# A gated embedding's product in seven block products instead of eight, on one Trainium2 core

## The chip, the cores and the metric

The kernel runs on one core of a Trainium2 chip. The metric is the time of one execution in device microseconds (us); lower is better. The engines are TensorE (PE, its weight loads PEld), VectorE (DVE), ScalarE (ACT), GpSimd (POOL) and the queue SP, which issues every DMA here.

## The reference, cut to what matters

One layer of an encoder for 1024 tokens of width 1024: two attention groups of eight heads each, then the output projection and a gated embedding for each token. All is float32. The last three lines are the part that the change concerns:

```
y = concat([sb_y, mla_y], axis=-1) @ w_out[i]
x = x + rms_norm(y, norm_post_g[i])

ple = rms_norm(p[i] @ w_ple[i], ple_norm_g[i])
x = x + ple * sigmoid(x @ w_ple_gate[i] + b_ple_gate[i])
```

The product `x @ w_ple_gate` is 1024x1024 by 1024x1024.

## The kernel before, in words

**Numbers in two parts.** TensorE multiplies in the type fp32r. To keep float32 accuracy each operand is split (`split`): a high part (a cast to fp32r) and a low part (the operand less its high part). A product then takes three matmuls: high by high, high by low, low by high. A matmul has a stationary operand of 128x128 (the tokens) and a moving one of up to 512 columns (the weight), and sums into a PSUM bank.

**A plan written before the program.** The kernel's code does not issue instructions: a `Recorder` notes each with the tiles that it reads and writes, and `schedule` then lists them for each engine by a model of their costs. An instruction's priority is its place in the recorded order, moved by a few constants (`LOW`, `AHEAD`, `URGENT`). SBUF is handed out by the same plan: 28 slots of 4 KB per partition named `u`, 10 named `f`, and 4 large ones named `h16` (rows show `h`). A slot can hold two halves of 2 KB. PSUM has 3 banks `a` and 5 banks `t`. Each engine, SP too, executes its list in order.

**The stages.** First come the input norm and projections, then the attention, in 32 units (`SEQ` lists 16 pairs), with projections, loads and the first of the output products woven between them (`FILL0`, `RATES`). At the end of the attention stands the tail, whose order is the list `TAIL`:

- a step `oT` (`e1`) is the output projection of token tile T (128 tokens): for each half of 512 columns 24 matmuls (8 blocks of the inner dimension, 3 each), then the norm and the residual; the weight lies split in the four `h16` slots. For tiles 4 to 7 the operand `ys1` lies in eight `u` slots until the last of them is done.
- a step `eT` is the gated embedding of tile T. `e2a` transposes the tile (8 transposes of 128x128 into two `t` banks) and splits it. `e2b` makes for each half 24 matmuls and then, in turn, DVE adds the bias, ACT takes the sigmoid, POOL multiplies by `pl` and adds to `x2`, and SP stores. In the last tile DVE does what POOL does elsewhere, and the last half is closed in two pieces of 256 columns.
- `wg_gen` loads the gate's weight in eight rows of blocks (512 KB each) and splits each: a cast of 128x1024 and a subtraction of 128x1024.

`choice(i)` gives an elementwise instruction to DVE where `SPLITS[i]` is 1 and to POOL where it is 0. All instructions are recorded through one line, L517, so groups in the profile are told apart by engine, operation and tile (`a` and `t` are PSUM; `u`, `f`, `h` SBUF).

Of the kernel before, what the change touches and what calls it, by code (L numbers as in the profile page):

```python
# [12 lines left out]
F32 = mybir.dt.float32  # L13
# [3 lines left out]
AF = mybir.ActivationFunctionType  # L17
ALU = mybir.AluOpType
# [5 lines left out]
D = 1024  # L24
NT = 8
# [85 lines left out]
class Access:  # L111
# [408 lines left out]
def block_kernel(ctx, tc, x, p, positions, norm_pre_g, w_in, q_norm_g, w_uq, kv_norm_g, w_ukv,  # L520
# [4 lines left out]
    PE, ACT, DVE, POOL, SP = R.PE, R.ACT, R.DVE, R.POOL, R.SP  # L525
# [12 lines left out]
    ps_a, ps_t, ps_s, ps_v, ps_l = (bank(k) for k in "atsvl")  # L538
# [30 lines left out]
    ident = const([128, 128], "ident")  # L569
# [17 lines left out]
    ple_d = dram([S, D], "ple_d")  # L587
# [11 lines left out]
    mm = PE.matmul  # L599
    half = [slice(0, 512), slice(512, 1024)]  # L600
# [17 lines left out]
    def choice(i):  # L618
        return DVE if SPLITS[i] else POOL

    def bcast(dst, src, n):
        SP.dma_start(dst, src[0:1, :].broadcast_to([128, n]))
        return dst

    def load_split(shape, src, name, leng=None, heng=None):

        raw = k4(shape, F32, name + "r")
        SP.dma_start(raw, src)
        wh, wl = k4(shape, name=name + "h"), k4(shape, name=name + "l")
        split(wh, wl, raw, leng=leng or POOL, heng=heng)  # L630
        return wh, wl
# [85 lines left out]
    gb = {}  # L717
# [512 lines left out]
    wo, wg = [[], []], [[], []]  # L1230

    def wo_gen():
        gb["post"] = bcast(k4(dt=F32, name="gb_post"), norm_post_g, D)
        for g in range(2):
            wo[0].append(h16(name="woh"))
            wo[1].append(h16(name="wol"))
            for k in range(4):
                raw = k4(dt=F32, name="wo_r")
                SP.dma_start(raw, w2o[:, 4 * g + k])
                split(wo[0][g][:, k], wo[1][g][:, k], raw, leng=choice(7 + k % 2))  # L1240
                yield 0.0

    def wg_gen():
        for k in range(8):
            h_, l_ = load_split((128, 1024), w2g[:, k], "wg", leng=choice(9 + k % 3))
            wg[0].append(h_)
            wg[1].append(l_)
            yield 0.0
        gb["b"] = bcast(k4(dt=F32, name="gb_b"), b_ple_gate, D)

    def big(lhs, w_h, w_l):

        def mms(ps, n):
            for kb in range(KB):
                lh, ll = lhs(kb)
                mm(ps, lh, w_h(kb, n), start=(kb == 0), stop=False)
                mm(ps, lh, w_l(kb, n), start=False, stop=False)
                mm(ps, ll, w_h(kb, n), start=False, stop=(kb == KB - 1))
                if kb in (2, 5):
                    yield 1.95  # L1260
            yield 1.3
        return mms

    x2s, x2t, yin = {}, {}, {}

    def y_load(t):
        ts = slice(t * 128, (t + 1) * 128)
        if t < 4:
            yt = [k4((128, 4, 2, 128), name="yin") for _ in range(2)]
            for g in range(2):  # L1270
                SP.dma_start(f(yt[g]), y_d[t, :, 4 * g:4 * g + 4])
            ys = lambda kb: [yt[kb // 4][:, kb % 4, a] for a in range(2)]
        else:
            ys = lambda kb: [ys1[kb][:, t - 4, a] for a in range(2)]
        xt = k4(dt=F32, name="x2")
        SP.dma_start(xt, x[0, ts, :])
        yin[t] = (ys, xt)

    def e1(t, keep):
        ys, xt = yin.pop(t)  # L1280
        mms = big(ys, lambda kb, n: wo[0][kb // 4][:, kb % 4, half[n]], lambda kb, n: wo[1][kb // 4][:, kb % 4, half[n]])
# [11 lines left out]
    def x2_load(t):  # L1293
        xt = k4(dt=F32, name="x2r")
        SP.dma_start(xt, x2_d[t * 128:(t + 1) * 128, :])
        x2s[t] = xt

    def e2a(t):
        x2 = x2s[t]
        xs = [[k2((128, 4, 128), name="x2t") for _ in range(2)] for _ in range(2)]  # L1300
        for g in range(2):
            ps = ps_t()
            for k in range(4):
                kb = g * 4 + k
                PE.transpose(ps[:, k * 128:(k + 1) * 128], x2[:, kb * 128:(kb + 1) * 128], ident)
            split(xs[0][g], xs[1][g], ps.rearrange("q (k n) -> q k n", k=4), heng=ACT)
        x2t[t] = xs

    def e2b(t):
        ts = slice(t * 128, (t + 1) * 128)  # L1310
        pl = k4(dt=F32, name="pl")
        SP.dma_start(pl, ple_d[ts, :])
        xs = x2t.pop(t)
        mms = big(lambda kb: [xs[a][kb // 4][:, kb % 4] for a in range(2)], lambda kb, n: wg[0][kb][:, half[n]], lambda kb, n: wg[1][kb][:, half[n]])
        x2 = x2s.pop(t)
        last = t == NT - 1
        eng = DVE if last else POOL
        for n in range(2):
            ps = ps_a()
            for _ in mms(ps, n):  # L1320
                pass
            w = 256 if last and n else 512
            for c0 in range(0, 512, w):
                v = slice(512 * n + c0, 512 * n + c0 + w)
                sg = k2((128, w), F32, "sgz")
                DVE.tensor_tensor(sg, ps[:, c0:c0 + w], gb["b"][:, v], ALU.add)
                ACT.activation(sg, sg, AF.Sigmoid)
                eng.tensor_tensor(pl[:, v], pl[:, v], sg, ALU.mult)
                eng.tensor_tensor(x2[:, v], x2[:, v], pl[:, v], ALU.add)
                SP.dma_start(out[0, ts, v], x2[:, v])  # L1330

# [3 lines left out]
    weave = Weaver(R)  # L1335
# [11 lines left out]

    for item in FILL0:
        fill(item)
# [19 lines left out]
    for u, (i, s) in enumerate(units):  # L1369
# [13 lines left out]
    for _ in range(5):  # L1383
        run_later(True)
    weave.drain()
    weave.add("wg", wg_gen(), False)
    R.front = True
    for t in range(N1, 4):
        for _ in e1_gen(t):
# [1 line left out]
    y_load(4)  # L1391
    R.front = False
    weave.drain()
    for step in TAIL:
        k, t = step[0], int(step[1])
        if k == "x":
            x2_load(t)
        elif k == "e":
            if t < 4 and t not in x2s:
                x2_load(t)  # L1400
            e2a(t)
            e2b(t)
        else:
            R.front = True
            if t + 1 < NT:
                y_load(t + 1)
            for _ in e1(t, True):
                pass
            R.front = False
    R.issue(tc)  # L1410

# [26 lines left out]
```

## Time and profile before

| what | value |
|---|---|
| median of 3 runs | 787.84 us (787.14 to 790.75) |
| the profiled execution, its own time | 793.85 us |
| its span, first to last instruction | 792.1 us |
| PE busy | 768.9 us (97%), 3948 matmuls |
| DVE, ACT, POOL busy | 537.6, 394.6, 330.1 us |
| granted TensorE clock, mean | 0.997 of full speed |

How to read it: the span is that of one execution under the profiler; the medians are of runs without it. A busy share is a mean over stages. Matmuls overlap one another, so the time that one costs in a row of many is read from start to start, not from its duration. A row of a group ends with the idle time before its instructions and what ended it.

### The profile page before, as it was taken

To read this page: it belongs to the slowest core of one execution; us is meant where nothing else is said; L and a number is where in the kernel's file an instruction comes from. 1 tells how busy PE (TensorE), PEld (TensorE's weight loads), DVE (VectorE), ACT (ScalarE), POOL (GpSimd) and SP (SyncE) were. 2 spreads that over 40 slices of the span, in tenths; PEclk is the share of its full clock that TensorE was granted. 3 is DMA by queue.
4 is the path that set the end of the run, shared out by engine and by line. 5 is a ranking of instruction groups with operands and counts; after the bars stand their busy time and mean duration, and the time that the engine had idled before them with its cause. 6 is when DMAs were issued, how large, how long until landed. Compare 5 with 4: busy or idle time off the path is not lost.

```text
span 792.1 us, 11714 instructions
## 1 busy us (share of the span) xinstructions
PE 768.9 (97%) x3948; PEld 634.2 (80%) x3948; DVE 537.6 (68%) x1006; ACT 394.6 (50%) x961; POOL 330.1 (42%) x318
## 2 busy tenths in 40 slices
PE   5999989999999999999998999999999999999997
PEld 3887879988888877888887787888888888888885
DVE  5775215489837869887987999999689886222222
ACT  5415124234526586676557777775966731211211
POOL 5654224102422259779877521010485140034342
PEclk9999999999999999999999999999999999999999
DMA  9544451158998636365545787685366365212311
GB/s 340 196 145 130 144 174 46 54 209 330 345 336 267 202 130 215 121 225 160 180 153 187 242 270 241 209 300 190 118 204 209 123 224 173 60 73 72 129 67 53
DMA packets 97166, 143.45 MB, mean 181 GB/s; under 512 B 7249, under 2 KB 54865, under 8 KB 97106
## 3 DMA queue, kind: packets, MB, share of 16 engines
q1 hardware_dynamic: 97106, 142.70, 53.9%
q8 instruction: 31, 0.51, 0.3%
q14 instruction: 29, 0.24, 0.1%
HBM read 96.02 MB, written 46.66 MB: 180 GB/s over the span
## 4 chain that ended last, share of the span: by engine, by line
PE 86%; DMA 6%; DVE 5%; ACT 2%; issue 1%; SPq 1%; DVEq 0%; ACTq 0%
PE a L517 61%; PE t L517 24%; DVE u L517 2%; DVE f L517 1%; ACT u L517 1%; DMA u<-q_d 1%; DMA f<-in_w_in_dram 1%; DMA y_d<-u 1%; DVE nm L517 1%; DMA q_d<-f 1%; SPq L517 1%; DMA u<-in_norm_pre_g_dram 1%; DMA k_d<-f 1%; ACT f L517 0%; DMA q_d<-u 0%
## 5 line engine op out<-in xcount | busy, mean ns | idle before, releaser
L517 POOL TENSOR_TENSOR u<-u,u 128x512 f32<-128x512 f32 (+17 forms) x155 | 216.1, 1405 | 165.6 <-ACT u L517 81.9
L517 PE MATMUL a<-h,f 128*128 128x512 f32 x864 | 239.6, 405 | 0.2 <-DVE f L517 0.2
L517 PE MATMUL a<-u,u 128*128 128x512 f32 (+2 forms) x762 | 188.4, 378 | 1.3 <-DVE u L517 0.6
L517 PEld LDWEIGHTS a<-h,f 128*128 128x128 f32 x864 | 155.7, 189 | 27.9 <-DVE f L517 0.5
L517 DVE TENSOR_TENSOR u<-t,u 128x512 fp32r<-128x512 f32 (+4 forms) x280 | 146.4, 554 | 25.2 <-ACT u L517 23.4
L517 PEld LDWEIGHTS a<-u,u 128*128 128x128 f32 x762 | 137.7, 188 | 29.1 <-DVE u L517 2.3
L517 ACT CAST u<-t 128x512 fp32r<-128x512 f32 (+3 forms) x256 | 113.4, 492 | 94.9 <-PE t L517 79.0
L517 PE MATMUL t<-u,u 128*128 128x512 f32 (+4 forms) x576 | 152.4, 370 | 4.5 <-DMA u<-q_d 4.2
L517 PE MATMUL t<-ident,u 128*128 128x128 f32 x792 | 126.5, 275 | 2.4 <-ACT u L517 1.7
L517 PEld LDWEIGHTS t<-u,u 128*128 128x128 f32 x576 | 102.7, 190 | 23.6 <-DMA u<-q_d 5.2
L517 PEld LDWEIGHTS t<-ident,u 128*128 128x128 f32 x792 | 97.3, 141 | 23.7 <-DVE u L517 5.1
L517 ACT ACTIVATE u<-t 128x384 f32<-128x384 f32 (+5 forms) x208 | 91.1, 518 | 46.3 <-PE t L517 35.0
L517 DVE TENSOR_TENSOR u<-a,u 64x512 f32<-64x512 f32 (+4 forms) x59 | 37.5, 642 | 80.5 <-PE a L517 67.3
L517 DVE TENSOR_TENSOR_SCAN u<-u 128x64 f32<-128x64 f32 (+3 forms) x64 | 69.4, 1094 | 27.4 <-ACT u L517 24.4
L517 ACT ACTIVATE f<-a 128x512 bf16<-128x512 f32 (+2 forms) x64 | 34.6, 542 | 81.1 <-PE a L517 70.5
L517 DVE TENSOR_TENSOR f<-a,f 128x512 f32<-128x512 f32 (+2 forms) x54 | 34.4, 644 | 51.4 <-ACT f L517 48.9
L517 PE MATMUL a<-h,u 128*128 128x512 f32 x288 | 68.9, 395 | 0.0
L517 ACT ACTIVATE u<-t,nms 128x384 f32<-128x384 f32 (+4 forms) x96 | 55.1, 581 | 21.7 <-DVE nms L517 19.5
L517 PEld LDWEIGHTS a<-h,u 128*128 128x128 f32 x288 | 53.9, 188 | 12.7 <-ACT u L517 0.3
L517 POOL MEMSET u<- 128x128 f32 x64 | 12.5, 208 | 106.0 <-PE t L517 38.2
L517 DVE TENSOR_REDUCE nm<-t 128x1 f32<-128x384 f32 (+4 forms) x96 | 51.8, 547 | 1.5 <-PE t L517 0.7
L517 PE MATMUL a<-u,h 128*128 128x512 f32 x192 | 51.7, 417 | 1.0 <-DVE h L517 1.0
(95 smaller groups left out, 710.5 us busy)
## 6 DMA issues: line engine op xcount, KB each, us to landing
u<-q_d SPq DMA_DIRECT2D x64, 256.0 KB, 4.6
u<-k_d SPq DMA_DIRECT2D x16, 512.0 KB, 6.3
u<-v_d SPq DMA_DIRECT2D x16, 512.0 KB, 5.3
f<-in_w_in_dram SPq DMA_DIRECT2D x14, 512.0 KB, 5.0
v_d<-u SPq DMA_DIRECT2D x12, 512.0 KB, 3.4
f<-in_x_dram SPq DMA_DIRECT2D x9, 512.0 KB, 6.5
k_d<-u SPq DMA_DIRECT2D x9, 512.0 KB, 3.7
q_d<-u SPq DMA_DIRECT2D x9, 512.0 KB, 4.8
```

The lines of the kernel that those rows point to most:

```text
L517: x["fn"](*[place(a) for a in x["args"]], **{k: place(a) for k, a in x["kw"].items()})
```

## The change

Two token tiles are now taken together. With the pair's operand in blocks A11, A12 (first tile, first and second half of the inner dimension), A21, A22 (second tile), and the weight's four 512x512 blocks B11, B12, B21, B22, the four output blocks are made of seven products of blocks instead of eight:

```
S1 = A21+A22   S2 = S1-A11   S3 = A11-A21   S4 = A12-S2
T1 = B12-B11   T2 = B22-T1   T3 = B22-B12   T4 = B21-T2
P1 = A11 B11   P2 = A12 B21   P3 = S4 B22   P4 = A22 T4   P5 = S1 T1   P6 = S2 T2   P7 = S3 T3
out11 = P1+P2            out12 = P1+P6+P5+P3
out21 = P1+P6+P7+P4      out22 = P1+P6+P7+P5
```

(P4's sign is in T4, which is recorded as B21-T2.) Each product is 12 matmuls of 512 columns (4 blocks, 3 matmuls each). Every sum is split in high and low again. The code, cut:

```
-TAIL = ("x1", "o4", "o5", "o6", "x2", "x3", "o7", "e3", "x0", "e4", "e0", "e1", "e5", "e2", "e6", "e7")
+TAIL = ("o4", "w1", "w2", "o5", "a4", "o6", "w3", "x1", "x0", "x2", "e4", "a0", "e0", "a6", "x3", "e6", "a2", "e2")
-SEQ = (... (2, 1), (5, 0), (5, 1), (7, 1), (4, 1), (1, 1), (6, 1))
+SEQ = (... (2, 1), (5, 0), (7, 1), (5, 1), (4, 1), (1, 1), (6, 1))
...
 wo_gen:
+        for n in range(2):
+            for a in wo:
+                a.append(h16((128, 8, 512), name="wo"))
             for k in range(4):
+                SP.dma_start(raw, w2o[:, 2 * k:2 * k + 2, half[n]])
...
+    def wg_part(i):
+        if i == 1:
+            for k in range(4):
+                SP.dma_start(raw, w2g[:, k::4, half[0]])
+                SP.dma_start(b12, w2g[:, k, half[1]])
+                split(h_, l_, raw, leng=choice(9), heng=ACT if SPLITS[10] else DVE)
+                choice(25).tensor_tensor(b12, b12, raw[:, 0], ALU.subtract)
+                split(t1[:, 0], t1[:, 1], b12, leng=choice(26), heng=ACT if SPLITS[10] else DVE)
+            return
+        h_, l_ = (h16((128, 4, 2, 512), name="wgs") for _ in range(2))
+        for a, nm in enumerate((("T4", "T2") if i == 2 else ("T3", "B22"))):
+            wg[nm] = [(h_[:, k, a], l_[:, k, a]) for k in range(4)]
+        for k in range(4):
+            SP.dma_start(ra, w2g[:, k::4, half[1]])
+            if i == 2:
+                SP.dma_start(rb, w2g[:, k::4, half[0]])
+                choice(27).tensor_tensor(ra[:, 0], ra[:, 0], rb[:, 0], ALU.subtract)
+                choice(28).tensor_tensor(ra[:, 1], ra[:, 1], ra[:, 0], ALU.subtract)
+                choice(29).tensor_tensor(ra[:, 0], rb[:, 1], ra[:, 1], ALU.subtract)
+            else:
+                choice(30).tensor_tensor(ra[:, 0], ra[:, 1], ra[:, 0], ALU.subtract)
+            split(h_[:, k], l_[:, k], ra, leng=choice(31 if i == 2 else 32), heng=ACT if SPLITS[11] else DVE)
...
 e2a (16 transposes of a pair into four t banks, then):
+        parts("A11", ps[0, 0], ACT, DVE)
+        ACT.copy(f11, ps[0, 0])
+        ACT.copy(f21, ps[1, 0])
+        DVE.tensor_tensor(s1, ps[1, 1], f21, ALU.add)
+        parts("S1", s1, ACT, choice(33))
+        parts("A12", ps[0, 1], ACT, DVE)
+        choice(34).tensor_tensor(s2, s1, f11, ALU.subtract)
+        parts("S2", s2, ACT, choice(35))
+        DVE.tensor_tensor(s4, ps[0, 1], s2, ALU.subtract)
+        parts("S4", s4, ACT, choice(36))
+        choice(37).tensor_tensor(f11, f11, f21, ALU.subtract)
+        parts("S3", f11, ACT, choice(38))
+        parts("A22", ps[1, 1], ACT, DVE)
...
 e2b (products in the order 1, 2, 6, 5, 3, 7, 4; close = bias or sum, sigmoid, times pl, plus x2, store):
+            if i == 4 and last:
+                for v in (slice(0, 256), slice(256, 512)):
+                    close(1, 0, product(xs, 4, v), w, w, v, DVE)
+            if i == 1:
+                ACT.copy(p1, ps)
+                DVE.tensor_tensor(p1b, ps, b0, ALU.add)
+            elif i == 2:
+                close(0, 0, ps, p1b, p1b)
+            elif i == 6:
+                DVE.tensor_tensor(u2, ps, p1, ALU.add)
+                choice(41).tensor_tensor(w, u2, b0, ALU.add)
+                choice(42).tensor_tensor(u2, u2, b1, ALU.add)
+            elif i == 5:
+                DVE.tensor_tensor(u2, ps, u2, ALU.add)
+            elif i == 3:
+                close(0, 1, ps, u2, p1)
+            elif i == 7:
+                DVE.tensor_tensor(w, ps, w, ALU.add)
+                close(1, 1, ps, u2, u2)
+            else:
+                close(1, 0, ps, w, w)
```

In the tail a step `wN` is `wg_part(N)`, `aT` is `e2a` and `eT` is `e2b` of the pair T, T+1; the pairs come in the order 4, 0, 6, 2, and `o6` and `o7` are recorded half by half in turn. DVE does choices 9, 25 to 27, 31, 35, 38, 41 and 42; POOL 28 to 30, 32 to 34, 36, 37, 39 and 40; the casts of the weight go to ACT. Besides `SEQ`, two neighbours change places in `FILL0` twice, `RATES` differs in four late entries, and three entries of `SPLITS` move instructions of the stages before the tail. `URGENT` changes as well.

TensorE, the last output half and the first products. Before, in the middle of the first tile of the gated embedding (the rows of one half, both operands in `u`):

```order
L517 MATMUL a_343<-u_6187,u_6580 128x512
L517 MATMUL a_343<-u_6213,u_6580 128x512
L517 MATMUL a_343<-u_6187,u_6580 128x512
L517 MATMUL a_343<-u_6258,u_6580 128x512
L517 MATMUL a_343<-u_6284,u_6580 128x512
```

Now, in the first pair, products 6 (its end), 5, and the beginnings of 3, 7 and 4; `u_6517` is S1, `u_6576` S4, `u_6586` S3, `u_6594` A22; `h_1` and `h_3` hold the high and low parts of T3 and B22, `h_0` and `h_2` those of T4 and T2:

```order
L517 MATMUL a_343<-h_0_202,u_6571 128x512
L517 MATMUL a_214<-u_6220,u_6517 128x512 x3
...
L517 MATMUL a_214<-u_6386,u_6517 128x512 x3
L517 MATMUL a_290<-h_1_391,u_6576 128x512
L517 MATMUL a_290<-h_3_402,u_6576 128x512
L517 MATMUL a_290<-h_1_391,u_6576 128x512 x2
L517 MATMUL a_290<-h_3_402,u_6576 128x512
L517 MATMUL a_290<-h_1_391,u_6576 128x512 x2
L517 MATMUL a_343<-h_1_391,u_6586 128x512
L517 MATMUL a_343<-h_3_402,u_6586 128x512
```

A half's 24 matmuls in one bank have become products of 12 in a bank each, and in this pair the products 3, 7 and 4 stand among one another, so that their third and fourth blocks come late.

POOL, from the end of the output projections on. Before (`hsr` is the norm of an output tile, the rows behind them the closing of the first tile):

```order
L517 TENSOR_TENSOR hsr_4225<-hsm_4169,nhalf 128x1
L517 TENSOR_TENSOR hsr_4006<-hsm_3985,nhalf 128x1
L517 TENSOR_TENSOR u_6534<-u_6534,u_6611 128x512
L517 TENSOR_TENSOR u_6402<-u_6402,u_6534 128x512
L517 TENSOR_TENSOR u_6534<-u_6534,u_6611 128x512
```

Now (`u_6597`, `u_6602`, `u_6611`, `u_6606` are the four blocks of the weight part w3; the rows to `h_3` make the low parts of T3 and B22; `u_6640` and `f_5971` close the pair's first tile):

```order
L517 TENSOR_TENSOR hsr_4225<-hsm_4169,nhalf 128x1
L517 TENSOR_TENSOR u_6597<-u_6597 128x512
L517 TENSOR_TENSOR hsr_4006<-hsm_3985,nhalf 128x1
L517 TENSOR_TENSOR u_6602<-u_6602 128x512
L517 TENSOR_TENSOR h_3_402<-u_6597,h_1_391 128x1024
L517 TENSOR_TENSOR h_3_402<-u_6602,h_1_391 128x1024
L517 TENSOR_TENSOR u_6611<-u_6611 128x512
L517 TENSOR_TENSOR u_6606<-u_6606 128x512
L517 TENSOR_TENSOR h_3_402<-u_6611,h_1_391 128x1024
L517 TENSOR_TENSOR h_3_402<-u_6606,h_1_391 128x1024
L517 TENSOR_TENSOR u_6640<-u_6640,u_6682 128x512
```

Four sums and four low parts of the weight now stand on POOL ahead of every closing.

TensorE at the program's end. Before, the last tile's last half:

```order
L517 MATMUL a_343<-u_6382,u_7019 128x512
L517 MATMUL a_343<-u_6393,u_7019 128x512
L517 MATMUL a_343<-u_6382,u_7026 128x512
L1434 UNCONDITIONAL_BRANCH
```

Now, the end of product 7 of the last pair and product 4 in two halves of 256 columns:

```order
L517 MATMUL a_343<-h_1_391,u_6963 128x512
L517 MATMUL a_214<-h_0_202,u_7118 128x256
L517 MATMUL a_214<-h_2_220,u_7118 128x256
L517 MATMUL a_214<-h_0_202,u_7118 128x256 x2
...
L517 MATMUL a_290<-h_2_220,u_7118 128x256
L517 MATMUL a_290<-h_0_202,u_7118 128x256
L1547 UNCONDITIONAL_BRANCH
```

The last 12 matmuls of 512 columns have become 24 of 256. In all, TensorE's list loses 60 matmuls of 512 columns and gains 24 of 256; the number of transposes stays.

## Rows read from the trace of the kernel before

**Rows 1.** The page: busy time, granted clock in 40 slices, chain that ended last.
```profile
PE 768.9 (97%) x3948; PEld 634.2 (80%) x3948; DVE 537.6 (68%) x1006; ACT 394.6 (50%) x961; POOL 330.1 (42%) x318
PEclk9999999999999999999999999999999999999999
PE 86%; DMA 6%; DVE 5%; ACT 2%; issue 1%; SPq 1%; DVEq 0%; ACTq 0%
```

**Rows 2.** Busy time of each engine in stretches of the tail, clock, DMA share, GB/s.
```profile
633.00:692.00 59.00, 58.98 (x276) 48.02 (x275) 35.85 (x53) 12.04 (x31) 10.62 (x8) 1.00 0.46 152
715.00:740.00 25.00, 25.00 (x126) 20.77 (x123) 6.12 (x10) 5.13 (x10) 10.33 (x8) 1.00 0.28 87
```

**Rows 3.** TensorE's longest waits in the whole span (in all, times, longest).
```profile
PE t L517 <- DMA u<-in_norm_pre_g_dram: 7.2, 1, 7.2
PE t L517 <- DMA u<-q_d: 4.2, 3, 1.9
```

**Rows 4.** TensorE in order of time, one tile of the gated embedding (start, us).
```profile
714.73 1.58 PE L517 MATMUL t<-ident,u 128*128 128x128 f32 x13
716.07 11.33 PE L517 MATMUL a<-u,u 128*128 128x512 f32 x48
727.24 0.49 PE L517 MATMUL t<-ident,u 128*128 128x128 f32 x3
727.49 11.32 PE L517 MATMUL a<-u,u 128*128 128x512 f32 x48
```

**Rows 5.** TensorE in order of time, matmuls of 256 columns in the attention.
```profile
461.56 0.64 PE L517 MATMUL a<-u,u 128*128 128x256 f32 x4
462.04 0.71 PE L517 MATMUL t<-ident,u 128*128 128x128 f32 x5
```

**Rows 6.** POOL and DVE in order of time, beside each other and POOL nearly alone.
```profile
648.77 1.22 DVE L517 TENSOR_TENSOR u<-u,u 128x1024 fp32r<-128x1024 f32 x1
648.87 2.26 POOL L517 TENSOR_TENSOR u<-u,u 128x512 f32<-128x512 f32 x1 [3.37 <-DVE hsm L517]
649.90 2.38 DVE L517 CAST u<-u 128x1024 fp32r<-128x1024 f32 x2
643.33 1.29 DVE L517 CAST u<-u 128x1024 fp32r<-128x1024 f32 x2
699.87 2.66 POOL L517 TENSOR_TENSOR u<-u,u 128x512 f32<-128x512 f32 x2 [6.79 <-ACT u L517]
```

**Rows 7.** Groups by form (busy us, mean ns of one, idle before).
```profile
L517 POOL TENSOR_TENSOR u<-u,u 128x512 f32<-128x512 f32 x46 | 68.6, 1494 | 110.7 <-ACT u L517 52.1 <-DVE u L517 41.5 <-DVE e L517 9.0
L517 POOL TENSOR_TENSOR f<-f,f 128x1024 fp32r<-128x1024 f32 x6 | 14.4, 2406 | 16.1 <-DVE f L517 7.2 <-ACT u L517 5.4 <-issue 3.6
L517 POOL TENSOR_TENSOR hsr<-hsm,nhalf 128x1 f32<-128x1 f32 x16 | 9.5, 594 | 53.0 <-DVE hsm L517 52.9
L517 DVE TENSOR_TENSOR u<-a,u 128x512 f32<-128x512 f32 x15 | 10.4, 692 | 64.5 <-PE a L517 64.5
L517 ACT CAST u<-t 128x512 fp32r<-128x512 f32 x128 | 71.4, 599 | 74.5 <-PE t L517 67.0 <-POOL u L517 3.7 <-DMA q_d<-u 1.8
L517 ACT ACTIVATE u<-u 128x512 f32<-128x512 f32 x15 | 9.5, 633 | 42.6 <-DVE u L517 42.6
```

**Rows 8.** DMA issues: count, KB each, median us from issue to landing.
```profile
u<-in_w_ple_gate_dram SPq DMA_DIRECT2D x8, 512.0 KB, 4.9
u<-in_x_dram SPq DMA_DIRECT2D x7, 512.0 KB, 8.4
```

**Rows 9.** The chain that ended last, its end (start, us).
```profile
775.65 11.13 PE a L517 x48
786.79 0.02 issue
788.48 0.34 DVE f L517
788.81 0.34 DVEq L1434
```

More of the change, by code (lines that the diff above doesn't have):

```diff
@@ L1229, in block_kernel @@
     w2g = w_ple_gate[0].rearrange("(kb q) n -> q kb n", q=128)
-    wo, wg = [[], []], [[], []]
+    wo = [[], []]
+    wg = {}
     def wo_gen():
         gb["post"] = bcast(k4(dt=F32, name="gb_post"), norm_post_g, D)
-        for g in range(2):
-            wo[0].append(h16(name="woh"))
-            wo[1].append(h16(name="wol"))
+        for n in range(2):
+            for a in wo:
+                a.append(h16((128, 8, 512), name="wo"))
             for k in range(4):
-                raw = k4(dt=F32, name="wo_r")
-                SP.dma_start(raw, w2o[:, 4 * g + k])
-                split(wo[0][g][:, k], wo[1][g][:, k], raw, leng=choice(7 + k % 2))
+                raw = k4((128, 2, 512), F32, name="wo_r")
+                SP.dma_start(raw, w2o[:, 2 * k:2 * k + 2, half[n]])
+                kk = slice(2 * k, 2 * k + 2)
+                split(wo[0][n][:, kk], wo[1][n][:, kk], raw, leng=choice(7 + k % 2))
@@ L1280, in e1 @@
         ys, xt = yin.pop(t)
-        mms = big(ys, lambda kb, n: wo[0][kb // 4][:, kb % 4, half[n]], lambda kb, n: wo[1][kb // 4][:, kb % 4, half[n]])
+        mms = big(ys, lambda kb, n: wo[0][n][:, kb], lambda kb, n: wo[1][n][:, kb])
         yg, rs = yield from half_norm(mms, gb["post"], "yg")
@@ L1298, in e2a @@
     def e2a(t):
[L1299 to L1312, printed above, removed]
-        xs = x2t.pop(t)
[L1314 to L1330, printed above, removed]
@@ new lines, in e2a, with parts @@
+        ps = {}
+        for i in range(2):
+            for g in range(2):
+                p_ = ps[i, g] = ps_t()
+                for k in range(4):
+                    kb = g * 4 + k
+                    PE.transpose(p_[:, k * 128:(k + 1) * 128], x2s[t + i][:, kb * 128:(kb + 1) * 128], ident)
+        out_ = {}
+        def parts(nm, src, heng, leng):
+            h_, l_ = k2(name="ah"), k2(name="al")
+            split(h_, l_, src, heng=heng, leng=leng)
+            out_[nm] = (h_, l_)
+        parts("A11", ps[0, 0], ACT, DVE)
@@ new lines, in e2a, with product @@
+        parts("S4", s4, ACT, choice(36))
+        choice(37).tensor_tensor(f11, f11, f21, ALU.subtract)
+        parts("S3", f11, ACT, choice(38))
+        parts("A22", ps[1, 1], ACT, DVE)
+        x2t[t] = out_
+    OPERANDS = {1: ("A11", "B11"), 2: ("A12", "B21"), 3: ("S4", "B22"), 4: ("A22", "T4"), 5: ("S1", "T1"),
+                6: ("S2", "T2"), 7: ("S3", "T3")}
+    def product(xs, i, v=slice(0, 512), ps=None):
+        ps = ps or ps_a()
+        a, b = OPERANDS[i]
+        for kb in range(4):
+            (ah, al), (bh, bl) = xs[a], wg[b][kb]
+            c = slice(kb * 128, kb * 128 + 128)
+            mm(ps[:, v], ah[:, c], bh[:, v], start=(kb == 0), stop=False)
+            mm(ps[:, v], ah[:, c], bl[:, v], start=False, stop=False)
+            mm(ps[:, v], al[:, c], bh[:, v], start=False, stop=(kb == 3))
+        return ps
@@ new lines, in e2b, with close @@
+    def e2b(t, order, last):
+        pl = []
+        for i in range(2):
+            pl.append(k4(dt=F32, name="pl"))
+            SP.dma_start(pl[i], ple_d[(t + i) * 128:(t + i + 1) * 128, :])
+        xs = x2t.pop(t)
+        x2 = [x2s.pop(t + i) for i in range(2)]
+        p1, p1b, u2, w = (k2(dt=F32, name=nm) for nm in ("p1", "p1b", "u2", "w"))
+        b0, b1 = (gb["b"][:, half[n]] for n in range(2))
+        def close(i, n, ps, part, sg, v=slice(0, 512), eng=None):
+            sg, part = sg[:, v], part[:, v]
+            DVE.tensor_tensor(sg, ps[:, v], part, ALU.add)
+            ACT.activation(sg, sg, AF.Sigmoid)
+            v = slice(512 * n + v.start, 512 * n + v.stop)
+            (eng or choice(39)).tensor_tensor(pl[i][:, v], pl[i][:, v], sg, ALU.mult)
+            (eng or choice(40)).tensor_tensor(x2[i][:, v], x2[i][:, v], pl[i][:, v], ALU.add)
+            SP.dma_start(out[0, (t + i) * 128:(t + i + 1) * 128, v], x2[i][:, v])
+        for i in order:
+            if i == 4 and last:
+                for v in (slice(0, 256), slice(256, 512)):
+                    close(1, 0, product(xs, 4, v), w, w, v, DVE)
+                continue
+            ps = product(xs, i)
+            if i == 1:
[16 more added lines that the diff above has]
+                close(1, 0, ps, w, w)
@@ L1393, in block_kernel @@
     weave.drain()
+    firsts = 0
     for step in TAIL:
@@ L1397, in block_kernel @@
             x2_load(t)
+        elif k == "w":
+            wg_part(t)
+        elif k == "a":
+            for i in range(2):
+                if t + i < 4 and t + i not in x2s:
+                    x2_load(t + i)
+            e2a(t)
         elif k == "e":
[L1399 to L1402, printed above, removed]
+            e2b(t, (1, 2, 6, 5, 3, 7, 4), firsts == 3)
+            firsts += 1
         else:
             R.front = True
[L1405 to L1408, printed above, removed]
+            if t < 6:
+                if t + 1 < NT:
+                    y_load(t + 1)
+                for _ in e1(t, True):
+                    pass
+            else:
+                if t not in yin:
+                    y_load(t)
+                y_load(7)
+                both = [e1(i, True) for i in (6, 7)]
+                for n in range(3):
+                    for g in both:
+                        for cost in g:
+                            if cost == 0.0:
+                                break
             R.front = False
```

35 lines of the change are left out of this document (22 added, 13 removed).

## The prediction, made before the changed kernel ran

> **What bounds the kernel now.** I read the page first: TensorE is busy 97% of the span, at full clock in every slice, and the chain that ended last is 86% TensorE [rows 1]. The reader is to see that no other engine is near it. Then the windows of the tail, which the change rewrites: from 633 to 692 us TensorE is busy 58.98 of 59.00, in a stretch of the gated embedding 25.00 of 25.00, while POOL has 10.33, DVE 6.12 and ACT 5.13 of that [rows 2]. Then TensorE's waits: the two largest, 7.2 us at the start and 4.2 in the attention, lie outside the tail [rows 3]. So the tail is a row of matmuls without a gap. What is taken off TensorE there comes off the end, as long as the others keep up.
>
> **The cost of a matmul here.** From 716.07 to 727.24 us stand 48 matmuls of 512 columns: 11.17 us, 0.2327 each from start to start. The 13 transposes before take 1.34 us and the 3 behind 0.25 [rows 4]: 16 for two tiles, 1.59 us. Four matmuls of 256 columns fill 461.56 to 462.04: 0.12 each [rows 5], half of a long one, so two short ones cost no more than one long one here.
>
> [...]
>
> **The change part by part.**
>
> *Removed from TensorE.* Each pair has 7 products of 12 matmuls, 84, where two tiles had 96. Over four pairs 48 go; the last product comes as 24 short ones. The order has 60 long ones fewer and 24 short ones more: 60 x 0.2327 - 24 x 0.12 = 13.96 - 2.88 = 11.1 us. Transposes stay at 64. A pair now takes 84 x 0.2327 + 1.59 = 21.1 us of TensorE.
>
> *Added for each pair on the others.* ACT: seven casts and three copies at 0.60 and four sigmoids at 0.63 [rows 7], 8.5 us. DVE: 17 instructions of 512 columns, 0.69 each [rows 7], 11.7 us. POOL: 12 instructions (two low parts, two sums, eight of the closings), 1.33 each when nearly alone (two in 2.66) [rows 6], 16.0 us. All three fit under 21.1, POOL with 5 us to spare. So they cost nothing as totals; what they can cost is latency.
>
> *The weight.* 9 MB are now loaded where 4 MB were (16 loads of 512 KB and 4 of 256 instead of 8), and 20 sums made. w1 and w2 lie beside the output projections of tiles 4 to 7: 192 matmuls, 44.7 us, where DMA was 46% busy and POOL 18% [rows 2]. They are cast into their places when those are free. The tight one is w3, at the first pair. Call t the end of the last output matmul. Its loads need slots that held the operand of the output projection; the first comes free 18 matmuls before t, at t-4.2, and a load lands 4.9 us later [rows 8], at t+0.7. POOL's list is then: a sum, a norm, a sum, two low parts, two sums, two low parts. With 1.33 a sum, 0.59 a norm and 2.41 a low part of 1024 columns [rows 7] the third low part ends at t + 0.7 + 4 x 1.33 + 0.59 + 3 x 2.41 = t+13.8, the fourth at t+16.2. TensorE has P1, P2, P6, P5 (48 matmuls) and then the first blocks of products 3, 7 and 4 (18) before it reads the third, 66 x 0.2327 = t+15.4, and ten more before the fourth, t+17.7. So 1.5 us of cover; I cost w3 at nothing, and if loads land as the slow ones did (8.4 us [rows 8]) and POOL's sums take their mean of 1.49 [rows 7], the third ends at t+18 and TensorE waits some 2.5 us.
>
> *Latency at each later pair.* Ahead of the second pair's P6 POOL must finish four closing instructions, S1's low part and S2, then ACT casts and DVE subtracts: counted from the first pair's end 0.7 + 6 x 1.33 + 0.6 + 0.7 = 10.0 us. On TensorE stand 29 transposes and 36 matmuls before that, 2.9 + 8.4 = 11.3. Cover 1.3 us; with POOL at 1.49 it is 0.3, at 2.26 (the instruction beside DVE [rows 6]) there is a wait of 4.3. Pairs 6 and 2 have similar lists. Bounds for all such waits together: 0 and 5 us, nearer the rows of a nearly free POOL; I take 1.5.
>
> *The end.* The last closing is the same as before, 256 columns on DVE, done 2.0 us behind the last matmul, the span ending 5.3 behind it at 792.1 [rows 9]. New is that product 7 is closed by POOL just before: 0.69 + 0.69 + 0.63 + 2.66 and some 0.2 of handing over, 4.9 us from its end, which lies 2.9 before TensorE's. It ends at 2.0 as well, and three stores follow one another on SP instead of two: 0.3 us, bounds 0 and 1.
>
> *Before the tail.* The output projection's weight now comes in halves of columns, as many bytes; half of its subtractions go from DVE to POOL. Two units change places and a few fills. TensorE's list is the same for its first 369 rows. Its gaps are 792.1 - 768.9 = 23.2 us, of which 7.2 at the start and 5.3 at the end are kept; the other 10.7, in waits of up to 1.9, are what a new order can change either way. I take nothing, bounds minus 3 and plus 3, a fraction of them.
>
> *Sum.* -11.1 + 1.5 + 0.3 = -9.3 us, on the profiled execution 793.85 - 9.3 = 784.5. That execution lies 6.0 us above the median of the runs, and the change touches nothing that I see in this difference; off the median, 787.84 - 9.3 = **778.5 us**.
>
> **The rivals.**
>
> *Late parts of the weight or sums.* For: covers of about 1.5 us; 9 MB; loads and stores share SP, whose list is in order. Against: in the tail before TensorE lost nothing behind similar chains. Price: 2.5 at w3 and about 1 at each of three pairs above the 1.5 taken, 4 us: 782.5 (to 784).
>
> *The attention's order loses.* For: it is another order, and the waits on q_d show that loads can be late [rows 3]. Against: TensorE was full there in most stretches. A loss of 4 to 7 us leaves 782 to 786, within 0.5% of before at its upper end. As likely is a gain of 3 and more: 775 and below.
>
> *POOL and DVE block one another, and POOL becomes the bound: slower.* A POOL instruction of 512 columns took 2.26 us where DVE subtracted two SBUF tiles, and DVE's two casts behind it 2.38 instead of 1.29 [rows 6]; the change adds 30 such instructions to POOL in the tail and 27 of two SBUF tiles to DVE. If each POOL instruction took 2.26, a pair would need 12 x 2.26 = 27.1 of POOL against TensorE's 21.1: 6.0 us lost at pairs 0 and 6, 1.5 at the last, which has 10; at the first, w3's POOL list would take 4 x 2.26 + 0.59 + 4 x 3.3 = 22.8 and end at t+23.5, 5.8 late. Together 19.3 - 11.1: 796. It decides from 21.1 / 12 = 1.76 us an instruction on, and eats the gain at about 2.1. Against: DVE has only four instructions of two SBUF tiles a pair, 2.8 us, so most POOL instructions meet none.
>
> [...]
>
> *It saves nothing, since weight loads bound the short matmuls.* Then 24 x (0.2327 - 0.12) = 2.7 us would come back. The weight loads are busy 80% [rows 1] and the short matmuls of the trace ran at 0.12 with a load each, so this is in the range alone.
>
> **How the numbers follow.** Forecast 60%, 775.5 to 781.5 by the attention's plus and minus 3. Late parts 17%, 781.5 to 785. The attention's order loses 8%, gains 6%. POOL as the bound or a like loss 9%. A measurement of this kernel can tell about 0.5%, 3.9 us, from no change: below 783.9 lie the forecast, the gain and most of the late parts, 0.80; between 783.9 and 791.8 the rest of these, 0.12; above, 0.08. The range takes the lowest forecast, 11.1 and another 3 us off, 774, and reaches up through the late parts to 786.
>
> **What would show it right or wrong.** TensorE's matmuls number 36 fewer, and its busy time falls by about 11 us. The tail from the first product to the end should show runs of 84 matmuls and 16 transposes in 21.1 us. Right on w3 if TensorE's waits show nothing above 1 us at the first pair's product 3. The forecast is wrong if waits of `a` on POOL, ACT or DVE sum to over 5 us behind the output projections, or if the part before the tail moved by more than 3 us.

## The result, and the profile after

The changed kernel took 780.75 us in the median (779.53 to 783.14, 5 runs) and the kernel before 788.13 on the same chip (787.14 to 790.79, 5 runs): ratio 0.9899, 95% interval 0.987 to 0.9927, so by the ratio 8.0 us less, between 5.8 and 10.2. A second measurement gave 780.2 against 790.24: 0.9886 [0.9862, 0.991], 9.0 us less, between 7.1 and 10.9. Forecast were 9.3 us less and 778.5.

The page of the changed kernel, busy times and chain, to be laid beside [rows 1]; its profiled execution took 780.85 us with a span of 778.8:

```profile
PE 756.4 (97%) x3912; PEld 624.7 (80%) x3912; DVE 569.8 (73%) x1041; ACT 422.1 (54%) x1001; POOL 395.1 (51%) x355
PE 81%; DMA 6%; DVE 5%; POOL 4%; ACT 2%; issue 1%; SPq 1%; POOLq 0%; DVEq 0%; ACTq 0%
```

TensorE has 36 matmuls fewer and 12.5 us less of busy time; its share, 97%, is as before. POOL, which was not in the chain, now holds 4% of it: the first sign of what the experiments found.

[rows 4] come from the execution that took 6.0 us more than its kernel's median. The kernel before, profiled again, took 790.03 us (span 788.3). The start of its gated embedding and its last matmuls, TensorE in order of time (start, duration, count):

```profile
686.66 1.04 PE L517 MATMUL t<-ident,u 128*128 128x128 f32 x8
771.59 11.37 PE L517 MATMUL a<-u,u 128*128 128x512 f32 x48
```

The same of the changed kernel, the first pair, the way into the second, the third pair and the end of the fourth; in brackets a wait and its releaser:

```profile
688.27 5.73 PE L517 MATMUL a<-u,u 128*128 128x512 f32 x24
693.84 2.96 PE L517 MATMUL a<-h,u 128*128 128x512 f32 x12
697.01 3.04 PE L517 MATMUL a<-u,u 128*128 128x512 f32 x12 [0.20 <-ACT u L517]
699.89 8.46 PE L517 MATMUL a<-h,u 128*128 128x512 f32 x36
708.20 1.91 PE L517 MATMUL t<-ident,u 128*128 128x128 f32 x16
709.86 6.27 PE L517 MATMUL a<-u,u 128*128 128x512 f32 x26
715.97 1.58 PE L517 MATMUL t<-ident,f 128*128 128x128 f32 x13
717.65 2.35 PE L517 MATMUL a<-u,u 128*128 128x512 f32 x9
...
731.81 5.74 PE L517 MATMUL a<-u,u 128*128 128x512 f32 x24
737.38 2.93 PE L517 MATMUL a<-h,u 128*128 128x512 f32 x12
740.15 2.96 PE L517 MATMUL a<-u,u 128*128 128x512 f32 x12
742.95 8.55 PE L517 MATMUL a<-h,u 128*128 128x512 f32 x36
751.34 1.69 PE L517 MATMUL t<-ident,u 128*128 128x128 f32 x14
...
764.37 8.58 PE L517 MATMUL a<-h,u 128*128 128x512 f32 x48
```

A pair reads as the products 1 and 2 (24 matmuls, weight in `u`), 6 (12, in `h`), 5 (12, `u`) and 3, 7, 4 (36, `h`). The third pair goes without a gap: 84 matmuls from 731.81 to 751.34, 0.2325 us each. From the first transpose to the last matmul's end the kernel before takes 686.66 to 782.96, 96.3 us; the changed one 688.27 to 772.95, 84.7, and its first 16 transposes (1.6 us) already lie in the output projections: 86.3 against 96.3. In these two executions the start is the same (688.27 less 1.6 is 686.7), so the gain lies in the tail, 10.0 us of it, and 0.5 goes back at the end: the span ends 5.85 us behind the last matmul instead of 5.3. That is 9.5 by the spans (788.3 to 778.8), 9.2 by the two executions' own times.

TensorE's waits in the whole span, against [rows 3] (us in all, times, longest), cut to three:

```profile
...
PE a L517 <- DMA u<-q_d: 1.2, 1, 1.2
PE t L517 <- DMA u<-q_d: 0.9, 2, 0.5
...
PE a L517 <- ACT u L517: 0.2, 1, 0.2
```

Behind the output projections the 0.2 us on ACT, at 697.01 above, is all that this view shows; waits of the weight loads, which overlap the matmuls (busy 624.7 us beside the matmuls' 756.4 in a span of 778.8), stand in a view of their own (below). The 4.2 us on `q_d` of [rows 3] are 2.1 here; they were 1.6 when the kernel before was profiled again, so they vary by themselves.

Busy time in stretches (TensorE, its loads, DVE, ACT, POOL; then clock, DMA share, GB/s), against [rows 2]: the output projections, then roughly one row for each pair.

```profile
633.00:692.00 59.00, 58.06 (x264) 46.89 (x263) 44.77 (x61) 26.24 (x48) 30.74 (x23) 1.00 0.52 173
...
688.00:710.00 22.00, 21.80 (x103) 17.64 (x103) 10.47 (x16) 9.15 (x13) 20.82 (x12) 1.00 0.55 211
710.00:732.00 22.00, 21.90 (x104) 17.74 (x104) 16.19 (x21) 11.27 (x21) 21.13 (x16) 1.00 0.31 101
732.00:752.00 20.00, 20.00 (x91) 16.21 (x91) 9.50 (x14) 4.14 (x8) 15.01 (x11) 1.00 0.44 145
752.00:773.00 21.00, 20.83 (x106) 17.07 (x104) 14.11 (x19) 7.88 (x15) 16.27 (x13) 1.00 0.29 100
```

TensorE is still full, but POOL, 10.33 of 25 us before, is busy 20.82 of 22 and 21.13 of 22 in the first two pairs. POOL there, and two rows of weight loads, that of TensorE's row at 717.65 and one in the last pair:

```profile
688.12 1.30 POOL L517 TENSOR_TENSOR u<-u 128x512 f32<-128x512 f32 x1 [1.19 <-PE a L517]
690.91 2.33 POOL L517 TENSOR_TENSOR u<-u 128x512 f32<-128x512 f32 x1
693.20 4.75 POOL L517 TENSOR_TENSOR h<-u,h 128x1024 fp32r<-128x1024 f32 x2
697.92 3.45 POOL L517 TENSOR_TENSOR u<-u 128x512 f32<-128x512 f32 x2
701.33 4.76 POOL L517 TENSOR_TENSOR h<-u,h 128x1024 fp32r<-128x1024 f32 x2
706.05 1.30 POOL L517 TENSOR_TENSOR u<-u,u 128x512 f32<-128x512 f32 x1
...
713.80 2.56 POOL L517 TENSOR_TENSOR f<-f,u 128x512 f32<-128x512 f32 x2
716.30 2.54 POOL L517 TENSOR_TENSOR u<-u,u 128x512 fp32r<-128x512 f32 x2
...
717.65 1.92 PEld L517 LDWEIGHTS a<-u,u 128*128 128x128 f32 x9 [0.34 <-POOL u L517]
...
753.61 4.94 PEld L517 LDWEIGHTS a<-u,u 128*128 128x128 f32 x22 [0.55 <-DVE u L517]
```

From 706.05 POOL makes all eight closing instructions of the first pair, then at 716.30 the low part of S1 for the second pair's product 5, done at about 717.6; TensorE's weight load stands waiting for it and goes on at 717.65. Thirteen transposes fill TensorE until then. That chain arrives exactly in time.

### The profile page after: what moved, and what is told of

Read it like the earlier page. It is cut to its first block, busy times and chain, and to the rows that moved or that the text cites. A ratio compares the mean times of both kernels' runs of the same rounds, so it can differ in the third digit from the quotient of the medians.

```text
span 778.8 us, 11830 instructions
## 1 busy us (share of the span) xinstructions
PE 756.4 (97%) x3912; PEld 624.7 (80%) x3912; DVE 569.8 (73%) x1041; ACT 422.1 (54%) x1001; POOL 395.1 (51%) x355
## 4 chain that ended last, share of the span: by engine, by line
PE 81%; DMA 6%; DVE 5%; POOL 4%; ACT 2%; issue 1%; SPq 1%; POOLq 0%; DVEq 0%; ACTq 0%
PE a L517 56%; PE t L517 24%; DVE u L517 3%; POOL u L517 2%; DMA u<-in_w_ple_gate_dram 2%; POOL h L517 1%; ACT u L517 1%; DMA u<-q_d 1%; DVE f L517 1%; DMA ple_d<-f 1%; DVE nm L517 1%; DMA q_d<-f 1%; DMA u<-in_norm_pre_g_dram 1%; SPq L517 1%; DMA f<-in_p_dram 1%
## 5 line engine op out<-in xcount | busy, mean ns | idle before, releaser
L517 POOL TENSOR_TENSOR u<-u,u 128x512 f32<-128x512 f32 (+18 forms) x171 | 241.1, 1426 | 116.9 <-DVE u L517 56.9
L517 DVE TENSOR_TENSOR u<-t,u 128x512 fp32r<-128x512 f32 (+4 forms) x284 | 149.3, 555 | 29.6 <-ACT u L517 23.9
L517 ACT CAST u<-t 128x512 fp32r<-128x512 f32 (+1 forms) x252 | 111.8, 490 | 65.0 <-PE t L517 46.2
L517 PE MATMUL a<-u,u 128*128 128x512 f32 (+2 forms) x522 | 133.1, 370 | 0.8 <-DVE f L517 0.3
L517 PE MATMUL a<-h,u 128*128 128x512 f32 (+1 forms) x492 | 115.5, 390 | 0.0
L517 PEld LDWEIGHTS a<-u,u 128*128 128x128 f32 x522 | 92.8, 188 | 18.9 <-DVE u L517 1.3
L517 PEld LDWEIGHTS a<-h,u 128*128 128x128 f32 x492 | 90.5, 188 | 20.4
L517 DVE TENSOR_TENSOR u<-a,u 64x512 f32<-64x512 f32 (+4 forms) x75 | 47.8, 651 | 40.6 <-PE a L517 18.5
L517 DVE TENSOR_TENSOR u<-u,u 128x512 fp32r<-128x512 f32 (+4 forms) x59 | 58.5, 1004 | 6.5 <-ACT u L517 3.6
L517 POOL TENSOR_TENSOR u<-u 128x512 f32<-128x512 f32 (+8 forms) x34 | 39.4, 1173 | 35.7 <-ACT u L517 18.7
```

Source lines behind the costliest of these rows:

```text
L517: x["fn"](*[place(a) for a in x["args"]], **{k: place(a) for k, a in x["kw"].items()})
```

## The experiments

Each ran beside the kernel before; times are compared through the ratio, since the medians of the kernel before lie between 788.13 and 790.24, and differences in us "by the ratios" are differences of two ratios times some 789 us. The stretch runs from the first product (of the kernel before: the first transpose) to the last matmul's end. The columns from the fourth on are those of the profiled executions (us):

| kernel | time | ratio to before [95%] | first product | last matmul ends | stretch | span ends behind it |
|---|---|---|---|---|---|---|
| before, again | 790.69 | 1.0013 [0.9993, 1.0032] | 686.66 (transposes) | 782.96 | 96.3 | 5.3 |
| changed | 780.75 | 0.9899 [0.987, 0.9927] | 688.27 | 772.95 | 84.7 | 5.9 |
| changed, again | 780.2 | 0.9886 [0.9862, 0.991] | 687.89 | 772.33 | 84.4 | 5.9 |
| eight products | 792.02 | 1.0022 [1.0004, 1.004] | 687.05 | 783.09 | 96.0 | 5.9 |
| old order before the tail | 782.01 | 0.9889 [0.9858, 0.992] | 692.52 | 776.90 | 84.4 | 5.9 |
| six products | 777.67 | 0.9841 [0.9813, 0.9869] | 689.17 | 770.82 | 81.7 | 5.9 |
| POOL four more | 792.85 | 1.0039 [1.0021, 1.0057] | 688.51 | 782.22 | 93.7 | 8.9 |
| POOL four, first pair | 787.4 | 0.9964 [0.9947, 0.9982] | 688.39 | 779.36 | 91.0 | 6.3 |
| POOL four, second pair | 782.0 | 0.99 [0.9874, 0.9926] | 688.70 | 773.31 | 84.6 | 6.2 |

### What are the matmuls worth: the changed kernel with product 5 done twice

The 12 matmuls of product 5 are issued a second time into the same bank, so TensorE has eight products and everything else is as changed.

```diff
             ps = product(xs, i)
+            if i == 5:
+                product(xs, i, ps=ps)
```

> The changed kernel with product 5 computed twice into the same bank (12 matmuls of 512 columns more a pair, 48 in all, as many as before the change; every sum, split and load of the change stays). Theory (in the tail TensorE alone sets the time, the additions on the other engines are hidden): 48 x 0.2327 = 11.2 us back, 780.75 + 11.2 = 791.9 us, some 3.5 us slower than the kernel before; that excess is then what the additions cost. Rival (much of the gain comes from the new order of the earlier stages): the same 11.2 us back as well, but without excess over the kernel before, if the earlier stages gave nothing the excess is the additions' cost. Rival (TensorE has slack behind late sums): under 8 us back.

792.02 us, by the ratio 1.7 above the kernel before (between 0.3 and 3.2), half of the 3.5 that were expected. The stretch is 11.3 longer than in the changed kernel for 48 matmuls of 0.2327 (11.2); by the ratios 9.7 and 10.7 us separate the two kernels. (This execution reached its tail 1.2 us earlier than the changed kernel's.) What the change adds costs 1.7 us with the matmuls put back, which also give the other engines more time; 1.5 and 0.3 were forecast.

### Do the tables before the tail matter: each half of the change alone

The changed tail with the tables of before (`SEQ`, `FILL0`, `RATES`, `URGENT`, four entries of `SPLITS`), and the kernel before with the new ones:

```diff
-SEQ = (... (5, 0), (7, 1), (5, 1), (4, 1), (1, 1), (6, 1))
+SEQ = (... (5, 0), (5, 1), (7, 1), (4, 1), (1, 1), (6, 1))
...
-URGENT = 56
+URGENT = 35
...
```

> The changed kernel's tail with the tables of before for the stages ahead of it (SEQ, FILL0, RATES, URGENT and the three SPLITS entries and the one of the output weight). Theory (the new tables are worth nothing, bounds -3 and +3): 780.75 within 1.5 us. Rival (the new tables gained some 3 us, as the two profiled executions' times up to the end of the output projections, 690.5 and 688.3 us with 1.6 us of transposes moved ahead, would have it): 784 to 785 us. Rival (they lost some 2 us): 778 to 779 us.

> The kernel before with the new tables for the stages ahead of the tail, its own tail kept. Theory (tables worth nothing): 788.1 within 1.5 us. Rival (they gain): 784 to 785 us. Rival (they lose): 790 us. The sign should be opposite to e2's.

> The kernel before, unchanged, for a second profiled execution. Theory (the first profiled execution, 793.85 us, 5.7 above the median of its runs, holds waits on q_d loads and a lower granted clock at 118 to 124 us that most executions do not have): time 788, and a profile in which TensorE's waits on q_d are 1 to 2 us instead of 4.2. Rival (the profiled execution of this kernel is always some 6 us longer): a profile of some 792 us of span again.

The new tables alone: 789.23 us, 0.9995 [0.9981, 1.0008]. The new tail alone: 0.9889 [0.9858, 0.992], as good as the whole change. The kernel run again: 1.0013. So the tables are worth nothing that can be measured, and the tail, with the loads of its weights, has all of it.

### What POOL has to spare

An idle multiplication of 512 columns on POOL (it rewrites a tile no longer needed) behind every closing of a pair that POOL does; twice in one kernel, once in the other.

```diff
             SP.dma_start(out[0, (t + i) * 128:(t + i + 1) * 128, v], x2[i][:, v])
+            if eng is None:
+                for _ in range(2):
+                    POOL.tensor_tensor(sg, sg, b0[:, 0:sg.shape[-1]], ALU.mult)
```

> The changed kernel with two more POOL instructions of 512 columns behind each closing, on a scratch tile that nobody reads: 20 instructions a pair instead of 12 (the last product's closing stays without). Theory (POOL becomes the bound once its instructions of a pair take over 21.1 us): 20 x 1.40 = 28.0, 6.9 us lost at pairs 0 and 6, some 5 at the last, and about 4 at the first: 15 to 22 us slower than the changed kernel, 796 to 803, slower than the kernel before. Rival (POOL's work stays hidden, its instructions off every chain to TensorE): under 4 us.

> As e8 with one more POOL instruction behind each closing instead of two: 16 a pair, at the 1.38 us that e8's had 22.1 us, one above TensorE's 21.1. Theory (the point from which POOL decides is 21.1 us a pair, 1.76 us for each of 12, and beyond it each pair loses the excess): 2 to 6 us slower than the changed kernel, 782 to 786. Rival (the covers of about 1.5 us at the sums are what matters, so POOL's extra 5.5 us a pair are lost nearly whole): 12 us or more slower. Rival (below the point nothing shows): no change.

808.11 us with two (ratio 1.0232), 27 above the changed kernel and more than was expected. 792.85 with one: 11 to 12 us more than the changed kernel by the ratios, for some 20 us of POOL work in four pairs (15 instructions of 1.3). The expectation of 2 to 6 rested on the 5 us to spare a pair; it fell, and its rival, a loss of 12 or more because the covers are short, came near. TensorE's waits in the tail, with two and then with one:

```profile
PE a L517 <- POOL u L517: 19.8, 3, 10.4
```

```profile
PE a L517 <- POOL u L517: 6.2, 3, 4.2
```

But which of them cost? Four of the fifteen by themselves, once behind the first pair's closings and once behind the second's (`if t == 4`, `if t == 0` in place of `if eng is None`):

> The changed kernel with four more 512-column GpSimd instructions, one behind each closing of the first pair of token tiles only (the second pair's closings as they are). Theory (GpSimd's sums for the next pair stand behind the closings of the pair before, so what counts is where the extra work stands): TensorE waits about 4.2 us before the second pair's product 5, as with eight instructions, and loses 1 to 2 us more at the lower clock that follows: 785 to 787 us. Rival (GpSimd's total counts): half of what the eight cost, about 786 us here and as much with the four behind the second pair's closings.

> The changed kernel with the same four more GpSimd instructions, only behind the second pair's closings. Theory: the third pair's sums come later, by which the eight cost 1.7 us at most in TensorE's waits, with the first pair's delay gone even less: 780 to 782 us. Rival (GpSimd's total counts): as the four behind the first pair's closings, about 786 us.

Behind the first pair they cost 5 to 6 us by the ratios (787.4 us), behind the second 0 to 1 (782.0). The same work, on the same engine, in neighbouring pairs: place counts, not total. In the first case POOL and TensorE in order of time, and the window behind the wait:

```profile
721.37 2.50 POOL L517 TENSOR_TENSOR u<-u,u 128x512 fp32r<-128x512 f32 x2
...
722.69 2.38 PE L517 MATMUL a<-u,u 128*128 128x512 f32 x5 [4.24 <-POOL u L517]
```

```profile
722.60:726.00 3.40, 3.31 (x8) 2.48 (x9) 2.11 (x4) 1.97 (x4) 3.32 (x4) 0.54 0.11 42
```

The wait stands where the changed kernel's weight load waited 0.34: the second pair's product 5, on S1's low part, now behind twelve instructions of the first pair. That low part begins at 721.37 instead of 716.30. With the four behind the second pair POOL is as full, and TensorE does not feel it:

```profile
710.00:735.00 25.00, 24.89 (x118) 20.20 (x117) 18.91 (x24) 13.02 (x24) 24.69 (x19) 1.00 0.27 93
```

There the third pair's first low part (the third of POOL's, in the recorded order two for each pair) begins at 726.76, against 726.54 in the changed kernel, with as many POOL instructions (six) between it and the second pair's first: the added work does not hold it up. The plan is made anew for each kernel, so other instructions move as well (13 of the last pair's transposes come earlier, at 740.37); what the place alone costs was not separated from that.

The two places together hold eight of the fifteen and lose 5 to 7 us; the other seven, behind the third and fourth pairs, were not run by themselves. With all fifteen, 11 to 12 us, POOL has almost no gap up to 777 us, a second wait stands before the last pair's product 5, and the span ends 8.9 us behind the last matmul instead of 5.9:

```profile
767.93 2.33 PE L517 MATMUL a<-u,u 128*128 128x512 f32 x9 [1.71 <-POOL u L517]
```

### Two attempts to take work from those chains

The two last operations of every closing on DVE (entries 39 and 40 of `SPLITS`):

```diff
-SPLITS = (... 1, 0, 0, 1, 0, 0, 1, 1)
+SPLITS = (... 1, 0, 0, 1, 1, 1, 1, 1)
```

> The changed kernel with all closings (the product with pl and the sum with x2, eight instructions a pair) on DVE instead of POOL. POOL has 4 instructions a pair left, DVE 25, at 0.69 us some 17 of TensorE's 21.1. Theory (in the changed kernel POOL is near its limit, 12 x 1.40 = 16.8 us a pair, but TensorE waits for it only 0.2 us): same time as the changed kernel within 1 us. Rival (POOL and DVE blocking one another is what the additions cost): 1.5 to 2 us faster than the changed kernel. Rival (DVE now stands between TensorE and its banks): 2 us or more slower.

781.16 us, 0.9895 [0.9873, 0.9917]: no difference from the changed kernel. TensorE's waits from 625 us on are 1.3 on DVE and 0.2 on POOL, where they were 0.9 on DVE and 0.2 on ACT. The chain was in time before and gained nothing by coming earlier, and DVE has the work now.

The other is the 0.9 us that TensorE waits on DVE at 637.45, in the output projections. DVE of the changed kernel, then TensorE:

```profile
634.25 0.69 DVE L517 TENSOR_TENSOR u<-u,u 128x512 f32<-128x512 f32 x1 [1.74 <-DMA u<-in_w_ple_gate_dram]
...
636.70 0.69 DVE L517 TENSOR_TENSOR u<-a,u 64x512 f32<-64x512 f32 x1
...
637.45 0.66 PE L517 MATMUL t<-ident,u 128*128 128x128 f32 x4 [0.94 <-DVE u L517]
```

T1's subtraction stands on the weight's load for 1.74 us, and behind it DVE's last attention output. The plan was told that the loads of the weight parts land 2.5 us later:

```diff
-                end = dma_free
+                end = dma_free + x["late"]
...
+            R.late = 2500.0
             wg_part(t)
+            R.late = 0.0
```

> The changed kernel with one constant in its plan: the loads of the gate's weight are taken to land 2.5 us later than its cost model says, so that the instructions that read them are listed later behind other work. Theory (in the profile after, DVE stood 1.7 us on the load of the first weight part at 634 us with the last attention unit's closing behind it, and TensorE waited 0.9 us for that): that wait goes, 0.9 us faster than the changed kernel, about 780 where that one is at 780.8. Rival (another wait takes its place): no change.

That attention output comes at 633.06 then, 3.6 us earlier, but from 625 us on TensorE waits for others (ACT 0.9 and 0.4, DVE 0.9): 781.8 us, 0.9899 [0.9879, 0.992]. The wait was traded for another.

> The changed kernel, unchanged, beside the others of this job. Theory (e1: the additions cost 1.7 us of the 11.2 that the matmuls give): 9.5 us below the kernel before, a ratio of 0.988. Rival (the first measurement's 0.9899 is the truth and e1's excess came from its own order): 8.0 us below.

Its result, 780.2 us, is the second measurement above.

### How much more there is: product 5 left out

Six products; out22 and out12 take P1 in its place, so two of four output blocks are not the reference's.

```diff
+            if i == 5:
+                DVE.tensor_tensor(u2, p1, u2, ALU.add)
+                continue
             ps = product(xs, i)
```

> The changed kernel without product 5 (its place in the sums takes product 1 again, so two of the four output blocks are not the reference's; sums and splits all stay): 72 matmuls a pair, 18.3 us of TensorE with the transposes, against POOL's 12 x 1.40 = 16.8. Theory (TensorE still sets the time, so a product is worth 11.2 us again): 780.5 - 11.2 = 769 us. Rival (POOL at 92% of a pair can't keep its covers): 771 to 775 us.

777.67 us; 769 was expected, 771 to 775 by the rival. 48 matmuls less, 11.2 us, and the stretch shortens by 3.0. TensorE's waits behind the output projections, the row behind the longest of them, and the clock there:

```profile
PE a L517 <- ACT u L517: 4.0, 2, 2.8
PE a L517 <- POOL h L517: 1.2, 2, 0.9
```

```profile
757.46 13.36 PE L517 MATMUL a<-h,u 128*128 128x512 f32 x60 [2.77 <-ACT u L517]
```

```profile
757.40:761.00 3.60, 3.54 (x10) 2.38 (x11) 2.83 (x3) 1.25 (x3) 3.60 (x3) 0.71 0.00 0
```

Of the lost 8.2 us, 5.2 are these waits. The row's 36 long and 24 short matmuls would take 11.3 us at the prices above and took 13.36, so about 2 more, an estimate, were lost behind the wait, where the clock was 0.71 over 3.6 us and 0.87 over the next 5.0; the last 1 was not traced. The seven products sit close to the limit of the chains over POOL and ACT.

## Why the prediction was right, and where a term was off

**The matmuls: right.** 11.1 us were forecast. With the matmuls put back the stretch grew by 11.3, a long one takes 0.2325, and the 24 short ones did not fall back to the price of long ones, the prediction's last rival: with 24 long ones they fill 8.58 us at 764.37, where 48 long ones would take 11.2.

**Waits: the size right, the place not.** 1.5 us were taken. The stretch got 10.0 shorter where the matmuls alone are 11.1, so 1.1 went to waits. Of these TensorE's view names the 0.2 at 697.01; the weight loads' view has two more, 0.34 on POOL at 717.65 and 0.55 on DVE at 753.61, together about the 1.1. The 0.9 at 637.45, on a load of the weight, was not foreseen: the prediction looked for late parts at their reader on TensorE, not for what stands behind them on DVE. Taken away, another wait came in its place.

**w3's cover: hardly any was left, no wait came.** Call t = 688.27 again. The third low part was forecast for t+13.8 and needed at t+15.4; it ended at 701.33 + 2.38 = 703.7, t+15.4. The fourth, forecast for t+16.2 and needed at t+17.7, ended at 706.09, t+17.8. The second block's load landed at 690.78, t+2.5, and its sum began at 690.91, t+2.6, as forecast (0.7 + 1.33 + 0.59). The 1.6 us were lost behind it: that sum took 2.33 instead of 1.33, and the next two 3.45 instead of 2.66. Beside both DVE worked on two SBUF tiles:

```profile
690.80 1.29 DVE L517 SCALAR_TENSOR_TENSOR f<-f,hsr,f 128x1024 f32<-128x1024 f32 x1 [0.66 <-DMA u<-in_w_ple_gate_dram]
...
697.76 2.45 DVE L517 TENSOR_TENSOR u<-u,u 128x512 f32<-128x512 f32 x2
```

TensorE shows no wait on POOL there. It was late itself: product 5 ended at 699.89, t+11.6, where 48 matmuls are 11.2, so some 0.4 of the 1.5 us of cover was left. The forecast of no wait above 1 us held; with six products, where TensorE comes to w3's parts 12 matmuls earlier, it waited 0.3 and 0.9 us for them.

**POOL's 5 us to spare: the step that was wrong.** "All three fit under 21.1, POOL with 5 us to spare. So they cost nothing as totals" counts a pair by itself. The first pair's closings stand behind w3's sums and low parts, so eight of them, not four, are ahead of the second pair's first low part. The cover there, 1.3 by the prediction, which looked at product 6, is none at product 5: the weight load waited 0.34 us for it, and with the old tables TensorE itself 0.16. Four more instructions at this place cost 5 to 6 us, at the next pair 0 to 1. The total was right (POOL is busy 15.0 and 16.3 us in the third and fourth pairs, 16.0 forecast). The forecast survived by luck: the chain comes out almost exactly even, which the prediction had not worked out.

**The slower rival: longer instructions show in the rows, their size is small.** POOL and DVE by form from 688 to 776 us (busy, mean ns), beside [rows 7]:

```profile
L517 POOL TENSOR_TENSOR u<-u,u 128x512 f32<-128x512 f32 x27 | 37.5, 1399 | 9.7 <-ACT u L517 9.5
...
L517 DVE TENSOR_TENSOR u<-a,u 128x512 f32<-128x512 f32 x31 | 20.6, 687 | 26.1 <-PE a L517 18.5 <-POOL h L517 3.6 <-POOL u L517 2.4
L517 DVE TENSOR_TENSOR u<-u,u 128x512 f32<-128x512 f32 x8 | 9.9, 1237 | 0.7 <-DMA out_dram<-u 0.5
```

DVE on two SBUF tiles takes 1.24 in the mean where the row at 634.25 had 0.69; with one tile in PSUM it is 0.69, as before in [rows 7]. POOL pays 1.40 in the mean where 1.33 was taken, far from the 1.76 at which the rival would decide. That the two engines lengthen each other's instructions is the author's reading of these rows: no run here took only their meeting away.

**The end: 0.5 instead of 0.3,** and not for the reason forecast. POOL, then DVE:

```profile
772.19 2.68 POOL L517 TENSOR_TENSOR u<-u,u 128x512 f32<-128x512 f32 x2 [0.72 <-ACT u L517]
...
772.48 1.26 DVE L517 TENSOR_TENSOR u<-u,u 128x256 f32<-128x256 f32 x1 [0.48 <-ACT u L517]
...
774.00 1.94 DVE L517 TENSOR_TENSOR u<-u,u 128x256 f32<-128x256 f32 x3
```

DVE is done at 775.94, 3.0 us behind the last matmul; before it was 2.4, since [rows 9] go to 789.15 with their last row, which the prediction's 2.0 left out. From there to the span's end it is 2.9 us, before 3.0, so the third store on SP, the forecast's reason, shows no cost. DVE's own end came later: its 256 columns at 772.48 took 1.26 us beside POOL's closing, where the kernel before took 0.43 for the same step (at 787.72).

**Before the tail: right.** Nothing was taken, and the tables measured nothing. To work off the median was right too: the kernel before, profiled again, was 3.8 us quicker than in the execution of the forecast.

## What to carry to other kernels

The 48 matmuls taken from a stretch in which TensorE hardly waited brought nearly their whole time, measured start to start (10.0 us of 11.1; put back, they cost 11.3), until the chains of the other engines came due: the next 48 brought 3.0 us of 11.2. Before calling such an engine free, follow its list in order past the stage's border: what it still owes from the stage before stands ahead of what the next one needs. The busy share did not show it here: from 710 to 735 us POOL was busy 24.30 of 25.00 us with the four instructions behind the first pair, which cost 5 to 6 us, and 24.69 with the four behind the second, which cost 0 to 1. To see how near the limit is, add work to the engine at one place and then at the next.

## What the runs showed of the hardware that was not expected

Two long waits of TensorE were followed by a lower granted clock: after 4.24 us of waiting, with four POOL instructions behind the first pair, it was 0.54 of full speed over the next 3.4 us, and after 2.77 us, with six products, 0.71 over 3.6 us. In the first of these kernels the stretch grew by 6.3 us, where TensorE's waits in it are 4.8. In the kernel with two extra POOL instructions, around a wait of 9.2 us, it was 0.81 over 27 us, the wait included:

```profile
720.00:747.00 27.00, 17.88 (x69) 14.08 (x70) 14.57 (x17) 8.28 (x14) 26.69 (x21) 0.81 0.13 48
```
